# Two layers of a hybrid encoder on one core: the order in which four stages begin and end, bank pools of depth two, attention's tiles placed anew

## The chip, the cores and the metric

The kernel runs on one core of a Trainium2 chip. The time is that of one execution on the device in microseconds; a time is given as the median of several runs with the lowest and the highest. The engines are TensorE (PE, with PEld for its weight loads), VectorE (DVE), ScalarE (ACT), GpSimd (POOL) and SyncE (SP), whose queue issues the DMA transfers here. Each works through its own queue in order and waits on semaphores for the others.

## The reference, cut to what matters

1024 prompt rows and 128 sample rows of width 1024 pass one HGRN2 layer and one layer of differential attention, each followed by an MLP with squared ReLU; every part has a norm ahead of it and one behind.

```python
def _sqrelu_mlp(x, w_up, w_down):
    return jnp.square(jax.nn.relu(x @ w_up)) @ w_down
...
for l in range(DEPTH):
    a = _rmsnorm(h, norm_g[l, 0])
    if l < N_A_LAYERS:
        m, s_new = _hgrn2(a, hg_state0[l], w_hgrn_in[l], lb_all[l], hgrn_onorm_g[l], w_hgrn_out[l], is_prompt)
    else:
        kv = _rmsnorm(h, kv_norm_g) @ w_kv
        m = _diff_attn(a, k_new, v_new, past_k, past_v, w_q, lam_p, subln_g, w_o, l)
    h = h + _rmsnorm(m, norm_g[l, 1])
    f = _sqrelu_mlp(_rmsnorm(h, norm_g[l, 2]), w_up[l], w_down[l])
    h = h + _rmsnorm(f, norm_g[l, 3])
```

D_MODEL is 1024, the inner width of the MLP 4096, there are 8 heads of width 128 in either layer.

## The kernel before

The rows are cut into nine blocks of 128: 0 to 7 are the prompt (NBP is 8, NP is 4, half of it), 8 the sample. Every matrix product in full precision is made of three products of TensorE (`mm3`): each operand is split into a high part (a cast on ScalarE, `whi`, `aTh`, `s0h`, `wh`) and what is left (a subtraction on VectorE, `wlo`, `aTl`, `s0l`, `wl`).

The stages follow one another: the start (x is loaded, normalised, transposed), HGRN with its heads, its output projection (`out_proj`), the MLP of layer 0 (`mlp_up`, `mlp_down`), attention, its output projection, the MLP of layer 1. A scheduler sets the order of the instructions on every engine and interleaves the end of a stage with the start of the next, so a line that is moved in one place moves rows on all engines.

*Start.* The string `START` sets the order: x0 loads block 0 of x, n0 makes its root and scales it with `norm_x` (L311), W0 loads weight tile 0 and splits it (L189, L190), s36 makes one root for blocks 3 to 5. `rstd_of` makes a root: a step on VectorE (L203), a square root on ScalarE, then L205, L207 or L209 and L210, and L211 on VectorE. `pq`, `pf` and `pi` are the products of the first head; ScalarE makes the sigmoids `sg` of `pq` and `sf` of `pf`.

*Output projection and up stage.* In `out_proj` each block's product `pm` gets a norm, gain and residual (L654, L657), a norm and gain for the MLP (L275), and its transposes. `pair_sums` makes sums and differences of blocks j and j+4 (L675 to L678, four steps of 128x512), as the MLP's product is done by a Winograd scheme with seven products P1 to P7 for eight. In `mlp_up` the weights of a pair of column blocks get four sums (`sums`, L732 to L735, steps of 128x512) and splits (L718); the operands S1, S3 and S4 are halves of the blocks, transposed and split (`s_ops`), and only then the big tiles of the projection are given back (`keep.close()`). The pair i = 0 has an order of its own: `P1 P2 T ops P6 P5 P7 smp P3 P4`. P2 is added in the bank X of P1, so it waits until ScalarE has copied P1 out (L786).

*Down stage.* `mlp_down` runs seven passes over its products `D`; the last one, P4, has two parts: over the chunks c, then over the blocks j with 24 products each. A block that is done goes to `finish` (square sum `jk`, gain L977, root, residual L979) and in layer 0 through a second norm to `to_operand`, which transposes it on TensorE (`S<-ident,aO`). GpSimd makes the gains of the blocks in `POOL_MLP`, VectorE the others.

*Attention.* The weights of head pairs come through `load_w`, with a gain: a list of gains is applied per row group by ScalarE and VectorE, an array is multiplied in by GpSimd first (L188). `pj` is the product for K, V and Q; the tiles of the stage are placed by the string in `Area(as_, "at", ...)`, with two turns for those with a number.

Of the kernel before, what the change touches and what calls it, by code (L numbers as in the profile page):

```python
# [19 lines left out]
P = 128  # L20
# [24 lines left out]
START = 'x0 g x1 x2 n0 n1 n2 r W0 W1 x3 x4 x5 W2 W3 x6 x7 x8 s36 s69'  # L45
# [22 lines left out]
def tile_kernel(ctx, tc, x_prompt, x_sample, cache_k, cache_v, state_hgrn, norm_g, w_hgrn_in,  # L68
# [252 lines left out]
    for x in START.split():  # L321
# [4 lines left out]
        elif x[0] == "n":  # L326
            stats([int(x[1])])
            norm_x(int(x[1]))
# [277 lines left out]
    def out_proj(w, gains, gain, o_src, osc, g_post, h_old, h_new, g_pre, order, W=None, early={}):  # L606

        keep = ExitStack()
        ts, blk = Area(keep, "ts", "ss ss8 rs_v rs_y rs_t t:8"), {}
        with ExitStack() as os_:  # L610
# [4 lines left out]
            def block(b):  # L615
                blk[b] = (ts.tile([P, D], F32, name="t", bufs=NBP) if b < NBP
                          else pp.tile([P, D], F32, name="t8", bufs=1))
                return blk[b]
# [13 lines left out]
            for b in order:  # L632
# [30 lines left out]
                done.add(b)  # L663
                if b < NBP and b ^ NP in done:
                    pair_sums(blk, b % NP, nc.vector if len(done) == NBP else nc.gpsimd)
# [19 lines left out]
    def mlp_up(l, blk, keep):  # L685
        wu = w_up[l].rearrange("(k p) n -> p k n", p=P)
        with ExitStack() as ms, ExitStack() as ls:
            R = Area(ms, "ur", "wst s0h s0l s1h s1l a4h a1h a1l a3h a3l a4l p1 u2 u3 c0 hs", side="right")
            B = Area(ms, "ub", "X U Y:3 Z:3", space=PSUM)
# [4 lines left out]
            def bank(tag):  # L694
                return B.tile([P, 512], F32, name=tag, bufs=1 if tag in "XU" else 3)

# [6 lines left out]
            def s_ops(name, src):  # L703
# [4 lines left out]
                for j in range(NP):  # L708
                    c = slice(j * P, (j + 1) * P)
                    half_T(src(j), h[:, :, c], lo[:, :, c], transpose, lambda n: bank("YZ"[j % 2]))  # L710
# [18 lines left out]
            def sums(st):  # L729
                b11, b12, b21, b22 = [st[:, 4 * r:4 * r + 4, c * P:(c + 1) * P] for r in range(2) for c in range(2)]  # L730
                tt = nc.gpsimd.tensor_tensor
# [43 lines left out]
            sums(st)  # L775
            tset = pend = nx = None
            for i in range(NFP):
                sets = (raw, tset)
                C = {}
                seq = "P1 P2 T ops P6 P5 P7 smp P3 P4" if i == 0 else "P1 P6 P2 P5 P7 smp P3 P4"  # L780
                for op in seq.split():
# [7 lines left out]
                    elif op == "P2":  # L789
                        prod(X, op, sets, False)  # L790
                        c = C["c11"] = cell()
                        nc.scalar.activation(c, X, AF.Relu)
# [6 lines left out]
                    elif op == "ops":  # L799
                        s_ops("S1", lambda j: blk[j + NP][:, 512:D])  # L800
                        s_ops("S3", lambda j: blk[j + NP][:, 0:512])
                        s_ops("S4", lambda j: blk[j][:, 512:D])
# [12 lines left out]
                    elif op == "P7":  # L815
                        prod(Y, op, sets, False)
                        u3 = R.tile([P, HT], F32, name="u3", bufs=1)
                        add(out=u3, in0=Y, in1=p1, op=ALU.add)
                        c = C["c22"] = cell()
                        add(out=c, in0=Z, in1=u3, op=ALU.add)  # L820
                        relu2(c)
                        store(c, "A22", i)
                        if nx is not None:
                            raw = split(nx, 2 * i + 2, [(r0, ca), (r1, ca)])
                            sums(nx)
# [47 lines left out]
    def mlp_down(l, g_post, h_old, h_new, last):  # L873
        wd = w_down[l].rearrange("(i s p) n -> s p i n", s=2, p=P)
        NC = NFP // 2
        with ExitStack() as ms:
            L = Area(ms, "dl", "hst:3 aO")
            R = Area(rest, "dr", "wsta:3 aE gb wstb:2 sst:2 ysm jk wh:4 wl:4 hb:2 ss rs_v rs_y rs_t", side="right")
# [88 lines left out]
            def finish(b, y):  # L967
# [8 lines left out]
                ss = sumsq(y, jk, R)  # L976
                (nc.gpsimd if b in POOL_MLP else nc.vector).tensor_tensor(out=y, in0=y, in1=gain[0], op=ALU.mult)  # L977
# [12 lines left out]
                late.append((b, y, step[0]))  # L990

# [28 lines left out]
            for pi, (p, an, bn, sh) in enumerate(PASSES):  # L1020
# [7 lines left out]
                for c in range(NC // 2 if tail else NC):  # L1028
# [21 lines left out]
                    if late and late[0][2] < step[0] - 2:  # L1050
                        to_operand(*late.pop(0)[:2], s_bank)
                    if todo and c % 3 == 1:
# [7 lines left out]
                if tail:  # L1060
                    for j in range(NP):
# [6 lines left out]
                        while late and late[0][0] < NP + j - 1:  # L1068
# [10 lines left out]
    def next_stage(place):  # L1079

        for i, (b, hf, rs) in enumerate(left):
# [8 lines left out]
             norm_g[0:1, 2], "whix5 wlox5 whix6 wlox6 whix7 wlox7 gb:2 hb:2 t8")  # L1090
# [19 lines left out]
    with ExitStack() as as_:  # L1110
        ap = Area(as_, "at", "kt q2 k8 KS0 V0 pK KT_s qq pf px ws so Qx KS1")
        next_stage(ap.tile([P, 2, D], F32, name="KS1", bufs=1))
        ap.pool("V1")
# [42 lines left out]

        def loads(h):
# [358 lines left out]
```

## Time and profile before

| what | value |
|---|---|
| median of 3 runs | 2996.42 us (2992.04 to 2997.12) |
| profiled execution | 2992.95 us |
| its span | 2991.2 us |
| mean granted clock of TensorE | 0.986 |
| PE, DVE, ACT, POOL busy | 2869.2, 1855.1, 1198.1, 705.8 us |

The profile is of one execution. The span goes from the first to the last recorded instruction; the execution's own time is 1.75 us longer. Busy times add up an engine's instructions. A timeline row gives the start, the duration, engine, line, operation, the tile written and those read, and in brackets how long the engine had been idle and what ended that. A tile's number is left out.

### The profile page before, as it was taken

How to read it: one execution, taken by the hardware profiler on the slowest of the kernel's cores; microseconds unless marked ns; L12 is line 12 of the kernel's file. 1: busy time of each engine (PE TensorE's matmuls, PEld its weight loads, DVE VectorE, ACT ScalarE, POOL GpSimd, SP SyncE). 2: the span in 40 equal slices, each digit the busy share in tenths (PEclk: the TensorE clock that was granted, in tenths of full speed). 3: DMA queues.
4: the chain of work that ended last, by engine and by line, in shares of the span. 5: the costliest groups of instructions: out<-in, count | busy, mean ns of one | idle time of the engine just before them, and what ended most of it. 6: DMA issues, size and time to landing. Idle time of an engine off the chain costs nothing.

```text
span 2991.2 us, 45326 instructions
## 1 busy us (share of the span) xinstructions
PE 2869.2 (96%) x16897; PEld 2506.5 (84%) x16897; DVE 1855.1 (62%) x3480; ACT 1198.1 (40%) x2570; POOL 705.8 (24%) x578
## 2 busy tenths in 40 slices
PE   7999999989899999999989999998989999999997
PEld 7999999978788887887778999997868888878876
DVE  7777777767644445455856565656684444545566
ACT  5222222243433334343545454555543333444432
POOL 1111111102445440123021020110133454402130
PEclk9999999999999999999999999999999999999999
DMA  4111111142243348687732121212332443677776
GB/s 136 53 52 52 52 52 52 52 155 91 78 150 129 126 151 299 209 270 253 274 102 79 43 86 41 85 51 85 118 109 85 142 138 125 205 252 251 263 239 232
DMA packets 337120, 405.27 MB, mean 135 GB/s; under 512 B 21081, under 2 KB 210690, under 8 KB 336898
## 3 DMA queue, kind: packets, MB, share of 16 engines
q1 hardware_dynamic: 336898, 402.37, 40.9%
q8 instruction: 133, 2.18, 0.3%
q14 instruction: 89, 0.73, 0.1%
HBM read 280.12 MB, written 122.16 MB: 134 GB/s over the span
## 4 chain that ended last, share of the span: by engine, by line
PE 40%; DVE 6%; issue 2%; ACT 2%; DMA 2%; POOL 0%; SPq 0%; DVEq 0%; ACTq 0%; POOLq 0%
PE D L238 10%; PE pj L238 9%; PE Y L238 5%; PE Z L238 3%; PE X L238 3%; PE sc L238 2%; PE po L238 2%; PE S L238 1%; PE U L238 1%; PE pt L235 1%; DMA wsta<-in_w_down_dram 1%; DVE wl L891 1%; DVE rs_t L207 0%; DVE wlo L190 0%; PE pm L281 0%
## 5 line engine op out<-in xcount | busy, mean ns | idle before, releaser
L238 PE MATMUL D<-wh,aTh 128*128 128x512 f32 x896 | 357.2, 399 | 9.4 <-DVE aO L1007 6.3
L238 PE MATMUL D<-wl,aTh 128*128 128x512 f32 x896 | 355.7, 397 | 0.6 <-DVE wl L891 0.6
L238 PE MATMUL D<-wh,aTl 128*128 128x512 f32 x896 | 355.3, 397 | 0.0
L891 DVE TENSOR_TENSOR aTl<-hst,aTh 128x1024 fp32r<-128x1024 f32 x112 | 143.9, 1291 | 210.8 <-ACT aTh L890 210.7
L238 PE MATMUL pj<-whi,aTh 128*128 128x256 f32 x864 | 255.2, 295 | 13.5 <-DVE V L1190 13.0
L238 PE MATMUL pj<-wlo,aTh 128*128 128x256 f32 x864 | 244.5, 283 | 5.3 <-DVE wlo L190 5.3
L238 PE MATMUL pj<-whi,aTl 128*128 128x256 f32 x864 | 244.6, 283 | 0.0
L890 ACT CAST aTh<-hst 128x1024 fp32r<-128x1024 f32 x112 | 116.6, 1047 | 275.5 <-PE D L238 237.2
L238 PEld LDWEIGHTS D<-wh,aTh 128*128 128x128 f32 x896 | 170.3, 190 | 50.9 <-issue 6.7
L238 PEld LDWEIGHTS D<-wl,aTh 128*128 128x128 f32 x896 | 170.3, 190 | 40.1 <-DVE wl L891 1.1
L238 PEld LDWEIGHTS D<-wh,aTl 128*128 128x128 f32 x896 | 170.1, 190 | 39.6
L238 PEld LDWEIGHTS pj<-whi,aTh 128*128 128x128 f32 x864 | 164.1, 190 | 22.2 <-DVE V L1190 15.8
L238 PEld LDWEIGHTS pj<-wlo,aTh 128*128 128x128 f32 x864 | 164.1, 190 | 6.2 <-DVE wlo L190 5.5
L283 PE MATMUL pi<-whi,aTl 128*128 128x256 f32 x576 | 166.9, 290 | 0.0
L281 PE MATMUL pi<-whi,aTh 128*128 128x256 f32 x576 | 165.7, 288 | 0.6 <-ACT sf L423 0.6
L282 PE MATMUL pi<-wlo,aTh 128*128 128x256 f32 x576 | 165.9, 288 | 0.0
L238 PEld LDWEIGHTS pj<-whi,aTl 128*128 128x128 f32 x864 | 163.9, 190 | 0.0
L891 DVE TENSOR_TENSOR wl<-wsta,wh 128x1024 fp32r<-128x1024 f32 x112 | 148.7, 1330 | 22.4 <-ACT wh L890 19.3
L753 POOL TENSOR_TENSOR c<-c 128x512 f32<-128x512 f32 x96 | 115.0, 1198 | 163.9 <-ACT c L752 163.2
L752 ACT ACTIVATE c<-c 128x512 f32<-128x512 f32 x96 | 60.7, 632 | 231.5 <-DVE c L820 193.1
L890 ACT CAST wh<-wsta 128x1024 fp32r<-128x1024 f32 x112 | 117.2, 1048 | 64.5 <-PE D L238 23.5
L1271 POOL COPY qq<-q 128x256 f32<-128x256 f32 x64 | 29.4, 460 | 397.4 <-PE pqT L235 273.2
(475 smaller groups left out, 8048.3 us busy)
## 6 DMA issues: line engine op xcount, KB each, us to landing
u_dr<-c SPq DMA_DIRECT2D x224, 256.0 KB, 4.3
hst<-u_dr SPq DMA_DIRECT2D x112, 512.0 KB, 4.7
wsta<-in_w_down_dram SPq DMA_DIRECT2D x112, 512.0 KB, 5.4
wst<-in_w_up_dram SPq DMA_DIRECT2D x32, 1024.0 KB, 6.0
wstb<-in_w_down_dram SPq DMA_DIRECT2D x32, 512.0 KB, 5.1
t_dr<-wsta SPq DMA_DIRECT2D x32, 512.0 KB, 3.9
wstb<-t_dr SPq DMA_DIRECT2D x32, 512.0 KB, 5.8
h_dr<-hb SPq DMA_DIRECT2D x27, 512.0 KB, 2.6
```

The costliest lines, as they stand in the source:

```text
L235: pin(nc.tensor.transpose(out, in_, ident))
L238: pin(nc.tensor.matmul(*a, **k))
L281: matmul(out, lh, rh, start=first, stop=False)
L282: matmul(out, lh, rl, start=False, stop=False)
L283: matmul(out, ll, rh, start=False, stop=last)
L752: nc.scalar.activation(c, c, AF.Relu)
L753: nc.gpsimd.tensor_tensor(out=c, in0=c, in1=c, op=ALU.mult)
L890: nc.scalar.copy(h, st)
L891: vt(out=lo, in0=st, in1=h.bitcast(F32), op=ALU.subtract)
L1271: nc.gpsimd.tensor_copy(qq, view(Qb[h, i][:], (h % 2) * P, [(64, 2), (0, 2), (1, 64)]))
```

## The change

It has these parts.

- Start: blocks 1 and 2 of x share one root (`s13`), and are scaled one after the other behind it (`m1 m2`).
- Bank pools of the stages outside the MLP are written without the number of turns (pools with two buffers).
- `out_proj`: nine tiles `t` for nine blocks; the sample block's transposes leave the projection and come in `mlp_up` behind S4; the pair sums of the last three blocks run on VectorE, not only the last.
- `mlp_up`, first pair: P2 has a bank of its own and is added to P1's copy on VectorE; the operands come one by one between the products; the first weight sums run on VectorE; the operands' transposes get two banks of their own (T). In every pair the sum for c22 no longer has a tile u3.
- `mlp_down`, last pass: a block's second half gets its square sum and its gain ahead of the first; both `aO` blocks' transposes come behind the last block's products.
- Attention: weights of head 0 are scaled per row group; the tiles are placed anew.

```diff
-START = 'x0 g x1 x2 n0 n1 n2 r W0 W1 x3 x4 x5 W2 W3 x6 x7 x8 s36 s69'
+START = 'x0 g x1 x2 n0 s13 m1 m2 r W0 W1 x3 x4 x5 W2 W3 x6 x7 x8 s36 s69'
...
-        ps[0] = Area(banks[0], "ps", "mm:2 aux:2 wide:2", space=PSUM)
+        ps[0] = Area(banks[0], "ps", "mm aux wide", space=PSUM)
...
-                if b < NP or b == NBP:
+                done.add(b)
+                if b == NBP:
+                    continue
+                if b < NP:
                     half_T(t[:, 0:512], aTh[:, b, 0:4], aTl[:, b, 0:4])
...
-                    pair_sums(blk, b % NP, nc.vector if len(done) == NBP else nc.gpsimd)
+                    pair_sums(blk, b % NP, nc.vector if len(done) > NBP - 3 else nc.gpsimd)
...
-            B = Area(ms, "ub", "X U Y:3 Z:3", space=PSUM)
+            B = Area(ms, "ub", "X U Y:2 Z:2 T:2", space=PSUM)
...
-            sums(st)
+            sums(st, nc.vector)
...
-                seq = "P1 P2 T ops P6 P5 P7 smp P3 P4" if i == 0 else "P1 P6 P2 P5 P7 smp P3 P4"
+                seq = "P1 P2 T S1 P6 S3 P5 S4 P7 smp P3 P4" if i == 0 else "P1 P6 P2 P5 P7 smp P3 P4"
...
-                        prod(X, op, sets, False)
                         c = C["c11"] = cell()
-                        nc.scalar.activation(c, X, AF.Relu)
+                        if i == 0:
+                            V = bank("Z")
+                            prod(V, op, sets, True)
+                            add(out=c, in0=V, in1=p1, op=ALU.add)
+                            nc.scalar.activation(c, c, AF.Relu)
+                        else:
+                            prod(X, op, sets, False)
+                            nc.scalar.activation(c, X, AF.Relu)
...
+                if b in half:
+                    ss = sumsq(y[:, 0], jk[:, 0], R)
+                    nc.vector.tensor_tensor(out=y[:, 0], in0=y[:, 0], in1=gain[0][:, 0], op=ALU.mult)
+                    nc.vector.tensor_tensor(out=ss, in0=ss, in1=half[b], op=ALU.add)
...
+            def second_half(b, y):
+
+                jk = R.tile([P, 2, 512], BF16, name="jk", bufs=1)
+                half[b] = R.tile([P, 1], F32, name="sh", bufs=NP)
+                nc.scalar.activation(jk[:, 0], y[:, 1], AF.Square, accum_out=half[b])
+                nc.gpsimd.tensor_tensor(out=y[:, 1], in0=y[:, 1], in1=gain[0][:, 1], op=ALU.mult)
...
-                        while late and late[0][0] < NP + j - 1:
+                        while late and (late[0][0] < NP or j == NP - 1):
                             to_operand(*late.pop(0)[:2], s_bank)
...
-        ap = Area(as_, "at", "kt q2 k8 KS0 V0 pK KT_s qq pf px ws so Qx KS1")
+        ap = Area(as_, "at", "q2 kt so KS0 V1 pf px ws KT_s V0 k8 Qx KS1")
...
-                gs = view(gv[:], G_KV + 4 * kh, [(1, 4), (0, 2 * P)])
+                gs = per_row(G_KV + 4 * kh) if h == 0 else view(gv[:], G_KV + 4 * kh, [(1, 4), (0, 2 * P)])
```

How the rows stand on the engines now is shown at three places; a row has the line, the operation, the tile written and those read.

VectorE at the start, before (xb_233 is block 1 of x, `wlo` the first weight tile's low part):

```order
L207 SCALAR_TENSOR_TENSOR rs_t<-rs_y,rs_v 128x1
L211 SCALAR_TENSOR_TENSOR rs_y<-rs_t,rs_y 128x1
L311 SCALAR_TENSOR_TENSOR xb_233<-xb_233,rs_y,g_229 128x1024
L203 TENSOR_SCALAR rs_v<-ss 128x1
L372 COPY tv<-pv 128x41
L265 TENSOR_TENSOR aTl<-pt,aTh 128x512 x2
L373 COPY gv<-tv 128x24
L374 TENSOR_SCALAR gv<-tv 128x1
L376 TENSOR_TENSOR mx<-tv 128x8
L190 TENSOR_TENSOR wlo<-wst,whi 128x1024
```

The same stretch after (xb_224 and xb_226 are blocks 1 and 2):

```order
L205 RECIPROCAL rs_y<-rs_y 128x2
L381 TENSOR_TENSOR e_412<-tv,mx 128x8 x2
L190 TENSOR_TENSOR wlo<-wst,whi 128x1024
L209 TENSOR_TENSOR rs_t<-rs_y 128x2
L190 TENSOR_TENSOR wlo<-wst,whi 128x1024
L210 TENSOR_TENSOR rs_t<-rs_t,rs_v 128x2
L211 SCALAR_TENSOR_TENSOR rs_y<-rs_t,rs_y 128x2
L311 SCALAR_TENSOR_TENSOR xb_224<-xb_224,rs_y,g_220 128x1024
L311 SCALAR_TENSOR_TENSOR xb_226<-xb_226,rs_y,g_220 128x1024
L203 TENSOR_SCALAR rs_v<-ss 128x3
```

Block 1's scaling stood ahead of both `wlo` rows, and now stands behind them with block 2's.

TensorE at the end of the down stage of layer 0, before (the products D of the last two blocks, and `pj`, attention's first product):

```order
L238 MATMUL D<-wl,aTh 128x512
L238 MATMUL D<-wh,aTl 128x512
L235 MATMUL S<-ident,aO 128x128 x8
L238 MATMUL D<-wh,aTh 128x512
...
L238 MATMUL D<-wl,aTh 128x512
L238 MATMUL D<-wh,aTl 128x512
L235 MATMUL S<-ident,aO 128x128 x8
L238 MATMUL pj<-whi,aTh 128x256
```

After, from the last products D to the first `pj`:

```order
L238 MATMUL D<-wh,aTl 128x512
L238 MATMUL D<-wh,aTh 128x512
L238 MATMUL D<-wl,aTh 128x512
L238 MATMUL D<-wh,aTl 128x512
L235 MATMUL S<-ident,aO 128x128 x16
L238 MATMUL pj<-whi,aTh 128x256
L238 MATMUL pj<-wlo,aTh 128x256
L238 MATMUL pj<-whi,aTl 128x256
```

The first eight transposes stood 24 products ahead of the second eight, and now all sixteen stand behind the last product.

VectorE at the start of the up stage of layer 1, before (L718 are the splits of the weights, L654, L657 and L275 steps of the projection):

```order
L654 SCALAR_TENSOR_TENSOR t<-pm,rs_y,gb 128x1024
L657 TENSOR_TENSOR hb<-hb,t 128x1024
L718 TENSOR_TENSOR s0l<-wst,s0h 128x4x128 x4
L203 TENSOR_SCALAR rs_v<-ss 128x1
L247 TENSOR_TENSOR aTl<-pt,aTh 128x512 x2
L205 RECIPROCAL rs_y<-rs_y 128x1
L207 SCALAR_TENSOR_TENSOR rs_t<-rs_y,rs_v 128x1
L211 SCALAR_TENSOR_TENSOR rs_y<-rs_t,rs_y 128x1
L275 SCALAR_TENSOR_TENSOR t<-hb,rs_y,gb 128x1024
L718 TENSOR_TENSOR s1l<-wst,s1h 128x1024
```

After (L735 to L738 are the four weight sums, L721 the splits, L655 and L658 the projection's):

```order
L721 TENSOR_TENSOR s0l<-wst,s0h 128x4x128
L658 TENSOR_TENSOR hb<-hb,t 128x1024
L721 TENSOR_TENSOR s0l<-wst,s0h 128x4x128 x3
L735 TENSOR_TENSOR wst<-wst 128x4x128
L247 TENSOR_TENSOR aTl<-pt,aTh 128x512
L203 TENSOR_SCALAR rs_v<-ss 128x1
L247 TENSOR_TENSOR aTl<-pt,aTh 128x512
L736 TENSOR_TENSOR wst<-wst 128x4x128
L205 RECIPROCAL rs_y<-rs_y 128x1
L737 TENSOR_TENSOR wst<-wst 128x4x128
L207 SCALAR_TENSOR_TENSOR rs_t<-rs_y,rs_v 128x1
L738 TENSOR_TENSOR wst<-wst 128x4x128
```

The four weight sums were in GpSimd's queue, and now stand between VectorE's splits and evictions.

## Rows read from the trace of the kernel before

**Rows 1.** The page's section 1: busy time (share of span), instructions.

```profile
PE 2869.2 (96%) x16897; PEld 2506.5 (84%) x16897; DVE 1855.1 (62%) x3480; ACT 1198.1 (40%) x2570; POOL 705.8 (24%) x578
```

**Rows 2.** Waits of PE: tile, line, releaser: us, times, longest.

```profile
PE pt L235 <- ACT junk L1344: 6.4, 5, 1.7
```

**Rows 3.** Timeline, DVE, start: start, duration (us), instruction, [idle before, releaser].

```profile
15.59 1.23 DVE L190 TENSOR_TENSOR wlo<-wst,whi 128x1024 fp32r<-128x1024 f32 x1 [0.96 <-ACT whi L189]
...
18.43 1.29 DVE L311 SCALAR_TENSOR_TENSOR xb<-xb,rs_y,g 128x1024 f32<-128x1024 f32 x1
...
21.14 0.18 DVE L205 RECIPROCAL rs_y<-rs_y 128x3 f32<-128x3 f32 x1 [1.11 <-ACT rs_y L204]
...
21.82 0.68 DVE L265 TENSOR_TENSOR aTl<-pt,aTh 128x512 fp32r<-128x512 f32 x1
22.42 3.67 DVE L311 SCALAR_TENSOR_TENSOR xb<-xb,rs_y,g 128x1024 f32<-128x1024 f32 x3
```

**Rows 4.** Timeline, PE, start.

```profile
22.56 0.69 PE L282 MATMUL pq<-aTl,whi 128*128 128x384 f32 x1
...
33.46 0.39 PE L281 MATMUL pi<-whi,aTh 128*128 128x256 f32 x1 [0.64 <-ACT sf L423]
```

**Rows 5.** Timeline, ACT, start.

```profile
29.97 1.28 ACT L415 ACT_TABLE_LOAD   x1
...
32.93 0.48 ACT L423 ACTIVATE sf<-pf 128x384 f32<-128x384 f32 x1
35.64 1.05 ACT L189 CAST whi<-wst 128x1024 fp32r<-128x1024 f32 x1 [2.23 <-DMA wst<-in_w_hgrn_in_dram]
```

**Rows 6.** Timeline, PE, up stage of layer 0, its start.

```profile
763.25 0.79 PE L238 MATMUL X<-aTh,s0h 128*128 128x512 f32 x1 [5.01 <-ACT p L786]
...
773.13 1.94 PE L242 MATMUL pt<-ident,t 128*128 128x128 f32 x8 [4.25 <-DVE t L275]
```

**Rows 7.** Timeline, DVE, the same place.

```profile
760.51 1.67 DVE L675 TENSOR_TENSOR t<-t 128x512 f32<-128x512 f32 x1
...
764.68 0.69 DVE L677 TENSOR_TENSOR t<-t 128x512 f32<-128x512 f32 x1
```

**Rows 8.** Windows: stretch, busy us (instructions) by engine, PEclk, DMA share, GB/s.

```profile
757.00:763.00 6.00, 1.24 (x8) 0.76 (x6) 6.00 (x9) 2.96 (x5) 3.86 (x3) 0.85 0.00 0
763.00:768.00 5.00, 4.75 (x11) 3.79 (x12) 5.00 (x7) 0.19 (x1) 0.00 (x0) 0.50 0.51 153
```

**Rows 9.** Timeline, PE, up stage of layer 1, its start.

```profile
2243.53 1.94 PE L242 MATMUL pt<-ident,t 128*128 128x128 f32 x8 [6.61 <-DVE t L275]
...
2255.36 0.47 PE L238 MATMUL Y<-aTh,s1h 128*128 128x512 f32 x1 [2.27 <-DVE a3l L247]
```

**Rows 10.** Windows, the same place, columns as in rows 8.

```profile
2240.00:2249.00 9.00, 4.92 (x22) 4.55 (x23) 4.77 (x10) 3.66 (x8) 0.00 (x0) 0.50 0.14 58
```

**Rows 11.** Timeline, PE, end of the down stage of layer 0, start of attention.

```profile
1491.92 0.50 PE L238 MATMUL D<-wl,aTh 128*128 128x512 f32 x1 [0.63 <-DVE wl L891]
...
1510.66 1.97 PE L235 MATMUL S<-ident,aO 128*128 128x128 f32 x8 [5.25 <-ACT aO L989]
...
1520.48 1.10 PE L235 MATMUL S<-ident,aO 128*128 128x128 f32 x8 [0.90 <-ACT aO L989]
...
1531.30 0.58 PE L238 MATMUL pj<-wlo,aTh 128*128 128x256 f32 x1 [5.29 <-DVE wlo L190]
```

**Rows 12.** Timeline, DVE, the same place.

```profile
1524.98 2.01 DVE L211 SCALAR_TENSOR_TENSOR rs_y<-rs_t,rs_y 128x1 f32<-128x1 f32 x1
```

**Rows 13.** Timeline, POOL, the same place.

```profile
1524.61 2.37 POOL L977 TENSOR_TENSOR aO<-aO,gb 128x1024 f32<-128x1024 f32 x1
```

**Rows 14.** Timeline, PE, end of layer 1.

```profile
2933.90 0.77 PE L238 MATMUL D<-wh,aTh 128*128 128x512 f32 x1 [6.29 <-DVE aO L1007]
```

**Rows 15.** Timeline, DVE, end of layer 1.

```profile
2930.74 1.28 DVE L979 SCALAR_TENSOR_TENSOR hb<-aE,rs_y,hb 128x1024 f32<-128x1024 f32 x1
...
2983.88 1.77 DVE L207 SCALAR_TENSOR_TENSOR rs_t<-rs_y,rs_v 128x1 f32<-128x1 f32 x1
```

More of the change, by code (lines that the diff above doesn't have):

```diff
@@ L327, in tile_kernel @@
             stats([int(x[1])])
+            norm_x(int(x[1]))
+        elif x[0] == "m":
             norm_x(int(x[1]))
@@ L608, in out_proj @@
         keep = ExitStack()
-        ts, blk = Area(keep, "ts", "ss ss8 rs_v rs_y rs_t t:8"), {}
+        ts, blk = Area(keep, "ts", "ss ss8 rs_v rs_y rs_t t:9"), {}
         with ExitStack() as os_:
@@ L615, in block @@
             def block(b):
-                blk[b] = (ts.tile([P, D], F32, name="t", bufs=NBP) if b < NBP
-                          else pp.tile([P, D], F32, name="t8", bufs=1))
+                blk[b] = ts.tile([P, D], F32, name="t")
                 return blk[b]
@@ L694, in bank @@
             def bank(tag):
-                return B.tile([P, 512], F32, name=tag, bufs=1 if tag in "XU" else 3)
+                return B.tile([P, 512], F32, name=tag, bufs=1)
             def a_op(name, k):
@@ L709, in s_ops @@
                     c = slice(j * P, (j + 1) * P)
-                    half_T(src(j), h[:, :, c], lo[:, :, c], transpose, lambda n: bank("YZ"[j % 2]))
+                    half_T(src(j), h[:, :, c], lo[:, :, c], transpose, lambda n: bank("T"))
             def split(st, n, parts):
@@ L798, in mlp_up @@
                         nx = load(1)
[L799 to L802, printed above, removed]
+                    elif op == "S1":
+                        s_ops(op, lambda j: blk[j + NP][:, 512:D])
+                    elif op == "S3":
+                        s_ops(op, lambda j: blk[j + NP][:, 0:512])
+                    elif op == "S4":
+                        s_ops(op, lambda j: blk[j][:, 512:D])
+                        for z in range(2):
+                            half_T(blk[NBP][:, z * 512:(z + 1) * 512], aTh[:, NBP, 4 * z:4 * z + 4],
+                                   aTl[:, NBP, 4 * z:4 * z + 4], transpose, lambda n: bank("T"))
                         keep.close()
@@ L816, in mlp_up @@
                         prod(Y, op, sets, False)
-                        u3 = R.tile([P, HT], F32, name="u3", bufs=1)
-                        add(out=u3, in0=Y, in1=p1, op=ALU.add)
                         c = C["c22"] = cell()
-                        add(out=c, in0=Z, in1=u3, op=ALU.add)
+                        add(out=c, in0=Y, in1=p1, op=ALU.add)
+                        add(out=c, in0=c, in1=Z, op=ALU.add)
                         relu2(c)
@@ L824, in mlp_up @@
                             raw = split(nx, 2 * i + 2, [(r0, ca), (r1, ca)])
-                            sums(nx)
+                            sums(nx, nc.gpsimd)
                     elif op == "smp":
@@ L990, in finish @@
                 late.append((b, y, step[0]))
+            half = {}
+            def second_half(b, y):
[3 more added lines that the diff above has]
+                nc.gpsimd.tensor_tensor(out=y[:, 1], in0=y[:, 1], in1=gain[0][:, 1], op=ALU.mult)
             def evac(p, j, o):
@@ L1051, in mlp_down @@
                         to_operand(*late.pop(0)[:2], s_bank)
+                    if tail:
+                        second_half(NP + c, aO[:, :, c])
                     if todo and c % 3 == 1:
@@ L1155, in tile_kernel, with per_row @@
         WT, ready = {}, set()
+        def per_row(g):
+            return [gv[:, g + i:g + i + 1] for i in range(4)]
         def loads(h):
```

21 lines of the change are left out of this document (10 added, 11 removed).

## The prediction

> **What bounds the kernel now.** I read the busy shares first: TensorE works 96% of the span, VectorE 62%, ScalarE 40%, GpSimd 24% [rows 1]. So nothing that is only work on another engine matters; time can come from the few places where TensorE stands still, and from what its clock loses behind a standstill. The second view is therefore TensorE's waits, and the third the timeline around each of the longer ones. Four places concern this change. At the start VectorE normalises the rows of x one block after another [rows 3] before the products `pq` and `pi` can run through [rows 4]. At the start of each up stage TensorE waits 5.01 and 4.25 us in layer 0 [rows 6], 6.61 and 2.27 us in layer 1 [rows 9]. At the end of layer 0's down stage and the start of attention it waits four times, 0.63, 5.25, 0.90 and 5.29 us [rows 11]. At the end of layer 1 it waits 6.29 us for an add of VectorE [rows 14]. A standstill also costs clock: after the 5.01 us in layer 0 the granted clock was 0.50, the 1.2 GHz level, over the next 5 us [rows 8].
>
> The profiled execution took 2992.95 us, 1.75 us of it outside the span, and is 3.5 us under the median of the three runs. I work on the profiled one and put the sum on the median.
>
> **The change part by part.**
>
> *Start, a loss.* Blocks 1 and 2 of x now share one root. In VectorE's new order the roots and the scaling of block 1 stand behind the `wlo` splits of the first two weight tiles; the second of these ran at 15.59 for 1.23 us, to 16.82 [rows 3]. Block 2 was scaled at 18.43 already, so it moves little; block 1, which was scaled ahead of the splits, now is scaled beside it, and all four evictions of blocks 1 and 2 queue behind. Ahead of block 2's first one now stand the root of blocks 3 to 5, which cannot start before ScalarE's answer at 21.14, the three small steps behind it (to about 21.9), three scalings that took 3.67 together [rows 3], and block 1's second eviction, 0.6: 21.9 + 3.7 + 0.6 = 26.2 instead of 21.82. `pq` needs that eviction for its second kind of product, which ran at 22.56 [rows 4]; it now runs at about 26.3, +3.8. In ScalarE's queue the casts of the next head's weights now stand ahead of the table load and the two sigmoids `sg` and `sf`. The second cast waited for its weights until 35.64 and took 1.05 [rows 5], so they start at about 36.6; the load takes 1.28 and a sigmoid 0.48, to 38.9, and the first `pi`, which waits on `sf`, comes at about 39.3 instead of 33.46 [rows 4, 5]. That is +5.8, and TensorE is full from there through HGRN, so it isn't regained. I take **+6**, from +4 (only the first shift counts) to +9 (the second weight tile's split is later too).
>
> *Two-buffer bank pools outside the MLP, HGRN's end, the output projection.* The pools keep their depth of two; TensorE doesn't wait for a bank there in the rows of its waits. **0**, from −1.5 to +2.
>
> *Up stage of layer 0.* The second product P2 now has a bank of its own, so it no longer waits for ScalarE's copy `p` of P1 (5.01 us, [rows 6]). But the next thing in TensorE's order is the transposes of a half that the pair sums make on VectorE, and these, L677 among them, ran until 765.37 [rows 7]; from 757 to 763 VectorE was busy 6.00 of 6.00 us [rows 8]. The change adds to that queue: three of four pair sums (four steps each) and the first weight sums (four steps) leave GpSimd for VectorE. Against this, VectorE's own steps there get shorter without GpSimd beside them: L675 took 1.67 us, where its like, L677, took 0.69 [rows 7]. Counting VectorE's new queue with 0.60 for such a step, L677 ends at about 764.05, so that TensorE stands from 758.1 to 764.1, 6.0 instead of 5.01, P2 runs at half clock as now, and behind it come three waits of 1 to 3 us instead of the 4.25. P7, the product after the operands, then starts where it started, by that count 0.2 us later. **0**, −3 to +3.
>
> *Up stage of layer 1.* The same code, other neighbours: no step of GpSimd stretches VectorE's here, and the long waits are the later ones, 6.61 for `t` of the last block's scaling and 2.27 for `a3l` [rows 9], with the half clock after the first: 0.50 from 2240 to 2249, where TensorE was busy 4.92 us [rows 10], half of it, 2.4, lost. In the new order the sample block's transposes, for which the 6.61 was waited, come only behind the operands S1, S3 and S4, and these have banks of their own (T). By the same count as in layer 0, P2 waits for L677 some 4.6 us, and the small waits behind it come to 1.6 more than the small ones of now: 6.61 + 2.27 + 2.4 = 11.3 off, 4.6 + 1.6 on. **−5**, −8 to −1.
>
> *Down stage of layer 0 into attention.* Two edits meet. The transposes of two blocks of `aO` now both stand behind the last block's 24 products, instead of one ahead of them. And the weights of the first head are scaled row by row by ScalarE and VectorE, not by GpSimd ahead of them. The 0.63 us went with GpSimd's scaling. The 5.25 us wait goes, the products close up, and the last ends at about 1510.6. Then the second block's operand is late instead: it was there at 1520.48 [rows 11]. The second halves of the sums of squares and of the gains now go ahead, and VectorE's small steps are no longer held as the 128x1 one of 2.01 us beside GpSimd's gain of 2.37 [rows 12, 13]; I put the operand at about 1516.7, a new wait of some 4 to 6 us. The 5.29 us for `wlo` shrinks to about 1.3, if the `w_dq` weights land as they did. Sum: 0.63 + 5.25 + 0.90 + 5.29 = 12.1 off, 5 + 1.3 on. **−6**, −11 (no new wait for the operand) to −1 (operand and weights as late as now: 12.1 off, 1520.5 − 1512 = 8 to 9 and 2 to 3 on).
>
> That four half-gains of `aO` are now GpSimd's in each down stage is a cost the rows only hint at. They show the pattern: a 128x1 step of VectorE with two inputs in SBUF took 2.01 us while GpSimd multiplied for 2.37 [rows 12, 13]. The Trainium skill, "SBUF — State Buffer", section "Who interferes with whom", says that the pair of ports which VectorE shares with GpSimd is an exclusive lock: an instruction of VectorE with two SBUF inputs and a reading one of GpSimd block each other for the whole instruction. The trace agrees here. By that rule the four halves could hold VectorE 4 x 1.2 = 4.8 us in each down stage, an estimate from half of GpSimd's 2.37, and that is the second rival below.
>
> *Attention's tiles and the output projection of layer 1.* TensorE's transposes of `p` wait on `junk` of ScalarE five times, 6.4 us together [rows 2]. The tile of these transposes takes its two banks in the other turn now, so that three of these waits end with an earlier release; I take 0.45 off each, −1.3, and −0.7 at attention's end, where tiles are placed anew. **−2**, −5 to +2 (a placed-anew tile that waits for an older one's reader).
>
> *End of layer 1.* The add that TensorE waited 6.29 us for stood behind one scaling with residual of 1.28 us [rows 14, 15], which now comes after it: −1.2. The last block's root was held 1.77 us [rows 15] beside a gain of GpSimd, which the halves take away: −1.3. The extra gains of GpSimd in the stretch before cost 0 to 3; I take 1. **−1.5**, −3.5 to +2.
>
> Sum: 6 + 0 + 0 − 5 − 6 − 2 − 1.5 = −8.5. On the median: 2996.4 − 8.5 = **2988**.
>
> **The rivals.** *More gain (2982).* If VectorE's queue in layer 0 closes up more than I count (each step beside GpSimd stretched as L675 was, 1.67 for 0.69), L677 ends 2 to 3 us sooner, TensorE stands under 4 us, P2 runs at full clock (2.5 us), and the up stage of layer 0 gives what layer 1's does: −14. For it: VectorE had no idle time there [rows 8], so every stretched step was paid. Against: as many steps come on as are relieved.
>
> *The tail gives little (2993).* GpSimd's half-gains hold VectorE 4.8 us, the second `aO` operand comes as late as before, and only the closing-up is left: −6 becomes −1, total −3.5, which is no difference that can be measured. For it: the rows of a step held 2.01 us; against: there are fewer GpSimd steps in that stretch altogether, since the weights' gains left it.
>
> *Slower (3003).* The eight VectorE steps that move there per up stage, and the two more sets of four ahead of them, cost TensorE in full: VectorE is the engine that ends its waits in both up stages, and 757 to 763 had no gap [rows 8]. Sixteen steps of 0.60 are 9.6 us. If two thirds lie ahead of L677, layer 0 costs +6 and layer 1, with its −5 gone, +4: 6 + 6 + 4 − 6 − 2 − 1.5 = +6.5. It decides from the point at which the pair sums of blocks 1 and 2 no longer fit beside the projection's products. Against: those products left VectorE waits there, and the relief on L675 is in the rows.
>
> **How the numbers follow.** Forecast 0.52, more gain 0.20, tail 0.16, slower 0.12. About 0.2%, 6 us, is what a measurement of this kernel can tell from no change, so the border to "faster" is 2990.4 and to "slower" 3002.4. The forecast's own spread of some 6 us puts 0.38 of its 0.52 under the border, 0.13 between, 0.01 above. With the rivals: faster 0.38 + 0.20 + 0.02 = 0.60, same 0.13 + 0.14 + 0.01 = 0.28, slower 0.01 + 0.11 = 0.12. The range runs from 2976, six under the greater gain's 2982, to 3000, where only the slower rival lies outside.
>
> **What would show it.** Start: the first `pi` at about 39 instead of 33.5; at 35 or under, the loss isn't there. Layer 0's up stage: TensorE's first wait names a VectorE step of the pair sums, not `p`, and is about 6 us; P7 at the same distance from X's first product as now. Layer 1's: no wait over 5 us. Tail: no `aO` wait among the D products, one of 4 to 6 behind them, `wlo` under 2. End: the D wait about 5 us, no root over 0.3 us. What would make me wrong: next-head weights that land earlier at the start, `w_dq` weights that land later in the tail, or VectorE held by GpSimd's halves in the down stages, which would show as D products that wait for `wl`.

## The result, and the profile after

The changed kernel takes 2962.1 us (2961.3 to 2965.4), the kernel before 2996.8 over the runs beside it; the ratio is 0.9889, with a 95% interval of 0.9872 to 0.9906. That is 33 us less by the ratio and 35 by the medians, where the forecast was 8.5 less and the range ended 14 us above the result. Direction and most of the steps came as forecast; one step, put down at zero, was worth more than all the others together.

The head of the page after, and its busy times:

```profile
span 2959.5 us, 45358 instructions
...
PE 2862.0 (97%) x16897; PEld 2502.0 (85%) x16897; DVE 1848.0 (62%) x3523; ACT 1207.4 (41%) x2597; POOL 673.0 (23%) x558
```

TensorE is 7.2 us less busy than before [rows 1], on the same number of instructions, and its share of the span is 97%. The rest of the 31.7 us that the span lost is standstill. The largest waits of TensorE after (total, times, longest, in us):

```profile
PE pt L242 <- DVE t L680: 10.5, 2, 5.8
PE pt L255 <- DVE xb L311: 8.5, 1, 8.5
...
PE S L235 <- ACT aO L1007: 5.6, 1, 5.6
PE D L238 <- DVE aO L1034: 5.0, 2, 4.3
...
PE pt L235 <- ACT junk L1375: 3.1, 4, 1.1
```

Gone is the wait that stood at the head of the same view before:

```profile
PE pj L238 <- DVE V L1190: 13.0, 9, 1.8
```

To see where the time went I set the start of the same instruction of TensorE in both traces side by side. A row says how late the changed kernel (or an experiment) is against the kernel before at that instruction, in us; the difference of two rows is what the stage between them won or lost. In the text these rows go by the short names `pi`, `pm`, `U`, `pj` and `D`. Each kernel has one profile, and a single stage is good to some 3 us: e4, which leaves attention as it was, shows it 2.6 us shorter than before.

| TensorE's instruction | before, at | changed | e1, banks alone | e2, changed without banks |
|---|---|---|---|---|
| first `pi` (start) | 33.46 | +5.45 | +0.47 | +5.28 |
| last `pi<-whi` (HGRN) | 614.50 | +2.68 | −2.80 | +5.05 |
| 382nd `pm`, 12 us ahead of the last of layer 0 | 742.12 | +2.63 | −3.80 | +3.03 |
| first `U<-s0h,aTl` (up stage's first pair, layer 0) | 790.79 | +6.93 | −3.41 | +9.98 |
| first `S<-aE` (late in the down stage) | 1443.07 | +7.41 | −5.06 | +10.34 |
| 17th `pj<-wlo` (attention's start) | 1535.73 | +0.55 | −2.10 | +3.50 |
| last `pj<-whi` (attention) | 2061.07 | −18.92 | −21.67 | −0.20 |
| last `pm<-whi` of layer 1 | 2225.80 | −25.36 | −22.01 | −1.16 |
| first `U<-s0h,aTl` of layer 1 | 2265.49 | −29.61 | −21.96 | −3.54 |
| last `D<-wh,aTh` | 2980.29 | −30.78 | −22.34 | −3.49 |

Between attention's start and its last `pj` alone the changed kernel wins 19.5 us. There the same products read like this before (TensorE's timeline; its last row is the one that waited, and below it stands VectorE's copy of V):

```profile
1617.35 0.71 PE L235 MATMUL pt<-ident,p 128*128 128x128 f32 x5
1617.82 0.36 PE L238 MATMUL pj<-whi,aTh 128*128 128x256 f32 x1
...
1618.50 0.28 PE L238 MATMUL pj<-whi,aTl 128*128 128x256 f32 x1
1620.34 0.38 PE L238 MATMUL pj<-whi,aTh 128*128 128x256 f32 x1 [1.57 <-DVE V L1190]
...
1620.01 0.28 DVE L1190 COPY V<-pj 128x128 f32<-128x128 f32 x1
```

and after:

```profile
1615.39 0.72 PE L235 MATMUL pt<-ident,p 128*128 128x128 f32 x5
1615.87 0.37 PE L238 MATMUL pj<-whi,aTh 128*128 128x256 f32 x1
...
1616.55 0.28 PE L238 MATMUL pj<-whi,aTl 128*128 128x256 f32 x1
1616.66 0.28 PE L238 MATMUL pj<-whi,aTh 128*128 128x256 f32 x1
...
1618.04 0.28 DVE L1221 COPY V<-pj 128x128 f32<-128x128 f32 x1
```

The product at 1620.34 waited 1.57 us for VectorE's copy of V out of the product right ahead of it. After, its like at 1616.66 follows the row at 1616.55 with nothing between, 1.4 us ahead of that copy: it no longer writes the tile that the copy still has to read.

### The profile page after: what moved, and what is told of

It is laid out like the page before. It is cut to its first block, busy times and chain, and to the rows that moved or that the text cites. A ratio compares the mean times of both kernels' runs of the same rounds, so it can differ in the third digit from the quotient of the medians.

```text
span 2959.5 us, 45358 instructions
## 1 busy us (share of the span) xinstructions
PE 2862.0 (97%) x16897; PEld 2502.0 (85%) x16897; DVE 1848.0 (62%) x3523; ACT 1207.4 (41%) x2597; POOL 673.0 (23%) x558
## 4 chain that ended last, share of the span: by engine, by line
PE 39%; DVE 6%; DMA 3%; issue 2%; ACT 2%; POOL 0%; SPq 0%; DVEq 0%; ACTq 0%; POOLq 0%
PE pj L238 9%; PE D L238 8%; PE Y L238 4%; PE Z L238 3%; PE X L238 3%; PE sc L238 2%; PE po L238 2%; PE U L238 1%; PE S L238 1%; DMA wsta<-in_w_down_dram 1%; PE pt L235 1%; DVE wl L904 1%; PE pm L281 0%; DVE hb L997 0%; PE pm L282 0%
```

## The experiments

The theory that I formed from this: the bank pools did it (A). The rival: the new places of attention's tiles did it (B), since V1 is among the tiles that moved. Twelve kernels were run; the times are medians, the ratios are to the kernel before beside them.

### The bank pools

**e1**, the kernel before with the bank pools alone:

```diff
-        ps[0] = Area(banks[0], "ps", "mm:2 aux:2 wide:2", space=PSUM)
+        ps[0] = Area(banks[0], "ps", "mm aux wide", space=PSUM)
```

> The kernel before with one edit: the bank pools outside the MLP as two-buffer pools (mm, aux, wide) instead of two turns each. Theory A (a two-buffer pool hands out the bank that was given back first, strict turns hand out the older one): TensorE's nine waits of pj for the copy of V, 13.0 us, go, the waits on junk shrink by about 3 us, HGRN and the second output projection gain some 2 to 6 us more: 2996 falls by 18 to 24 us. Theory B (the placing of attention's tiles did that, the banks nothing): within 2 us of before, the nine waits still there.

Measured: 2973.8 us, ratio 0.9926 (0.9914 to 0.9939), 21 us less. The nine waits are gone, and of the waits on `junk` half is left:

```profile
PE pt L235 <- ACT junk L1344: 3.2, 4, 1.1
```

**e2**, the changed kernel with that line as before:

> The changed kernel with the turns of before put back for mm, aux and wide. Theory A: it loses what the banks gave, 18 to 24 us of the changed kernel's gain of 34, and the waits of pj for V are back with about 13 us; the start's loss no longer shrinks from 5.4 to 2.7 us through HGRN. Theory B: within 3 us of the changed kernel.

Measured: 2987.7 us, ratio 0.9973 (0.9961 to 0.9985). The waits are back, at nearly their old size:

```profile
PE pj L238 <- DVE V L1221: 12.7, 9, 1.8
...
PE pt L235 <- ACT junk L1375: 6.4, 5, 1.7
```

Theory B has fallen: without the pools the rest of the change, tiles included, is 7 to 8 us. That is close to the 8.5 that the prediction gave for all of it.

**e3**, the kernel before with the pool for `mm` alone, `"mm aux:2 wide:2"`:

> The kernel before with the two-buffer pool for mm alone, aux and wide in turns. Theory A with the price at pj: 12 to 14 us less than before, the waits on junk (6.4 us) stay. If the gain is that of all three pools (18 to 24), the junk waits were the projections' doing; if it is under 5, the banks of aux or wide carry it.

Measured: 2981.5 us, ratio 0.9953 (0.9940 to 0.9967). No wait of `pj` for V is listed, and the one on `junk` stands:

```profile
PE pt L235 <- ACT junk L1344: 6.0, 4, 1.7
```

**e9**, the kernel before with the pool for `aux` alone, `"mm:2 aux wide:2"`:

> The kernel before with the two-buffer pool for aux alone. The three pools together gave 21 us, mm alone 13. Theory A (the transposes pt and the small tiles of attention get the bank that was given back first): the waits on junk, 6.4 us, fall by some 3, and the 3.3 us by which HGRN was shorter with all three pools are aux's too: 5 to 8 us less than before. Rival: these belong to wide or only come together with mm: within 3 us of before.

Measured: 2989.7 us, ratio 0.9983 (0.9974 to 0.9992). Here it is the other way round:

```profile
PE pj L238 <- DVE V L1190: 12.9, 9, 1.8
...
PE pt L235 <- ACT junk L1344: 3.4, 5, 1.1
```

So 13 to 14 us are the bank of `pj`, 5 to 7 the banks of the small tiles, and they add up to e1's 21. On top of the other edits the same line gives more, 25 us (the changed kernel against e2): 15.8 in attention, 5.5 in the second output projection, 2.7 in the up stage of layer 0 and 2.5 in HGRN. Of e9's gain 2.9 us arise in HGRN, like e1's 2.8 (the last `pi` comes at 611.57 and 611.70 instead of 614.50), while with `mm` alone it comes at 614.72. So HGRN's part belongs to `aux`. Which instructions of HGRN got shorter I can't say: TensorE's list of waits names none there over 0.6 us in either trace.

What the pools change is which bank the next tile gets. With two turns, `pj`, `kps` (the four transposes of `stack`, which fall into the middle of a projection) and the next `pj` get first, second, first: the product must wait until VectorE has copied V out of the product right ahead of it. In eight of the nine places TensorE's timeline has the four `kps` inside the product right ahead of the one that waits. With the pool that one starts ahead of the copy, as the rows above show, so it has another bank. That a two-buffer pool gives out the bank that was given back first is my reading of this; e3 shows that the line does it, and at which wait.

### Where attention's tiles lie

**e8**, the changed kernel with the string of places as before:

```diff
-        ap = Area(as_, "at", "q2 kt so KS0 V1 pf px ws KT_s V0 k8 Qx KS1")
+        ap = Area(as_, "at", "kt q2 k8 KS0 V0 pK KT_s qq pf px ws so Qx KS1")
...
+        ap.pool("V1")
```

> The changed kernel with attention's tiles placed as before. Theory A: no wait of pj for V comes back, within 2 us of the changed kernel between attention's start and its end; what the placing gave is at attention's end and in the output projection, at most 4 us. Theory B (tiles carry it): 10 us or more lost.

Measured: 2969.3 us, ratio 0.9909 (0.9893 to 0.9926), 5 to 7 us more than the changed kernel. At the last `pj` it is 2.6 us ahead of the changed kernel, so inside attention the places cost nothing; at the last `pm` of layer 1 it is 5.6 behind. The second output projection thus gives 8.2 us, twice what I had allowed at most. The queue of SyncE shows what happens there. Its issues of the last weights of the projection and of the first of the up stage, in e8:

```profile
2119.27 0.38 SPq L174 DMA_DIRECT2D wst<-in_w_do_dram  x1
...
2128.50 0.38 SPq L729 DMA_DIRECT2D wst<-in_w_up_dram  x1
```

and in the changed kernel:

```profile
2103.75 0.38 SPq L174 DMA_DIRECT2D wst<-in_w_do_dram  x1
...
2119.53 0.43 SPq L729 DMA_DIRECT2D wst<-in_w_up_dram  x1
```

The first is issued 15.5 us earlier, the second 9. As I read it, both go to tiles that lie where attention's tiles lay, and wait for the last reader of what was there. The kernel before issued them at 2134.35 and 2144.20, 73 and 83 us behind its last `pj`; the changed one does so 62 and 77 behind, e8 80 and 89. What these loads give isn't separated. Of the 8.2 us, 1.8 come within 20 us of the last `pj`, ahead of these loads, where the mean granted clock over 25 us was 0.80 in e8 and 0.93 in the changed kernel. The other 6.4 come among the projection's own products, where TensorE waits 5.5 us in all for steps of VectorE in e8, and 1.0 in the changed kernel; that VectorE is earlier there because the weights come earlier is not shown. And the places give this only together with the pools: in e2, which has the new places and the old turns, the second projection is just 1.0 us shorter than before.

### The start

**e5**, the changed kernel with the start of before (`n0 n1 n2` instead of `n0 s13 m1 m2`):

> The changed kernel with the start of before (blocks 1 and 2 of x with a root each). Theory A (the start's shift of 5.4 us lasts, and the shrinking to 2.7 through HGRN is the bank pools' gain): 5 us less than the changed kernel, 2957. Rival (HGRN takes the shift up, TensorE waits there less when it is late): 2 to 3 us less, or nothing.

Measured: 2955.9 us, ratio 0.9861 (0.9846 to 0.9876). The first `pi` comes 4.8 us earlier than in the changed kernel, the last one 5.4, the last `D` 5.9. The rival, that HGRN takes the shift up, has fallen; e2 says the same, whose shift was 5.28 at the first `pi` and 5.05 at the last.

### The up stage of layer 0

**e4**, the kernel before with only the edits of the up stage and of the projection's end:

> The kernel before with only the edits of the up stage and of the output projection's end (own bank for P2, T banks, operands between the products, nine tiles t, pair sums and first weight sums on VectorE). By the changed kernel's trace: +4 us in the up stage of layer 0, -4 in layer 1's, sum within 2 us of before. If the prediction's count were right: 0 and -5. Rival: the second output projection's gain (about -4 between attention's end and the up stage) is from the nine tiles t, then -4 to -6 in all.

Measured: 2996.8 us, ratio 1.0008 (0.9999 to 1.0017): nothing. By the landmarks it is 7.2 us later in the up stage of layer 0 (−0.25 at the 382nd `pm`, +6.96 at the first `U`) and 3.1 earlier in layer 1's (+10.51 to +7.38). Its profile is of an execution 5 us above its median. But e2, whose profile is near its median, loses 7.0 in the same stage, and the kernels with the pools (e5, e8, e10, e11) 3.8 to 4.4 like the changed one: without the pools the up stage of layer 0 costs 7 us, with them 4.

**e6**, the changed kernel, layer 0's up stage as before, layer 1's as changed (each edited place asks for the layer; two of them):

```diff
-            sums(st, nc.vector)
+            sums(st, nc.vector if l else nc.gpsimd)
...
-                        if i == 0:
+                        if i == 0 and l:
                             V = bank("Z")
```

> The changed kernel with the up stage of layer 0 as before (order of the first pair, P2 in P1's bank, no T banks, sums and pair sums on GpSimd, sample block's transposes in the projection), layer 1 as changed. Theory A (the edits lose 4 to 7 us in layer 0 by the pair sums and by the half clock behind three waits, and win 4 in layer 1): 4 to 7 us less than the changed kernel, 2956. By the prediction's count, 0 within 3 us.

Measured: 2957.8 us, ratio 0.9870 (0.9855 to 0.9885), 4 us less than the changed kernel; the gain stands between the 382nd `pm` (−0.5) and the first `U` (−4.8). The nine tiles `t` and the sum without u3 stay in both layers.

**e7**, both of them, the old start and the old up stage of layer 0:

> The two of them together. If the two losses add: 9 to 12 us less than the changed kernel, 2951. If the time gained is given back at the down stage's weights or at attention's start, 5 or less.

Measured: 2951.6 us, ratio 0.9851 (0.9836 to 0.9866), the lowest of all the medians (e5's interval overlaps with it): 10 us less than the changed kernel. At the first `U` the two add up in full, 10.5 us; at attention's start 8.4 are left and at the last `D` 6.9. The profiled runs' spans differ by 7.2 (2952.3 against 2959.5).

**e12**, the changed kernel with the old start, and in layer 0 only the first weight sums back on GpSimd (`sums(st, nc.vector if l else nc.gpsimd)`):

> The changed kernel with the start of before, and in layer 0 only the first weight sums back on GpSimd (four steps of 128x512; VectorE runs them in 0.68 each). Theory A (VectorE's queue ahead of the pair sums sets the wait there): the wait for L680's like falls from 5.8 by 2 to 3 us, and the up stage of layer 0 ends 2 to 4 us earlier than with old start alone (2956). Rival (GpSimd beside VectorE stretches the steps by as much): within 1.5 us, steps of VectorE over 1 us where 0.68 was.

Measured: 2957.3 us, ratio 0.9872 (0.9854 to 0.9889); e5 has 2955.9. The rival holds. TensorE's wait for the pair sum is 5.98 us, with another of 1.43 ahead of it, not 3 (5.79 in e5). VectorE's timeline says why:

```profile
751.83 2.41 DVE L275 SCALAR_TENSOR_TENSOR t<-hb,rs_y,gb 128x1024 f32<-128x1024 f32 x1
...
754.22 2.23 DVE L719 TENSOR_TENSOR s1l<-wst,s1h 128x1024 fp32r<-128x1024 f32 x1
...
757.76 1.21 DVE L719 TENSOR_TENSOR s1l<-wst,s1h 128x1024 fp32r<-128x1024 f32 x1
```

The step L275 took 2.41 us and the first split L719 2.23, the second 1.21. GpSimd in the same stretch:

```profile
751.87 1.28 POOL L735 TENSOR_TENSOR wst<-wst 128x512 f32<-128x512 f32 x1 [0.69 <-DVE rs_y L211]
753.23 2.13 POOL L736 TENSOR_TENSOR wst<-wst 128x512 f32<-128x512 f32 x1
```

Each long step of VectorE lies beside a sum of GpSimd, as L675 did before [rows 7, 8]. What VectorE loses by taking the sums, four steps of 0.68, it loses about as much of beside GpSimd when it doesn't: 2.1 us in these two steps alone. This is the exclusive port pair that the Trainium skill states ("SBUF — State Buffer", section "Who interferes with whom"), and the trace agrees: 2.23 against 1.21 for two halves of the same split.

### The end of the down stage

**e10**, the changed kernel with the last pass of the down stage as before:

```diff
-                    if tail:
-                        second_half(NP + c, aO[:, :, c])
...
-                        while late and (late[0][0] < NP or j == NP - 1):
+                        while late and late[0][0] < NP + j - 1:
```

> The changed kernel with the down stage's last pass as before (no halves ahead, one block's transposes among the products). The prediction put the last pass and the weights' scaling at -6 together and layer 1's end at -1.5. If the order of the transposes and the halves carry it: 4 to 6 us more than the changed kernel, with aO waits of 5 and 1 us among the products. If the weights' scaling carries it: within 2 us.

Measured: 2968.0 us, ratio 0.9912 (0.9896 to 0.9928), 6 us more than the changed kernel. The place of the old transposes is back, with 4.27 us of waiting for `aO` among the products, and the wait for `wlo` is 4.52 us instead of 2.26. By attention's start 3.7 us are lost (from −0.88 at the 225th `D` to +2.86 at the 17th `pj<-wlo`, against the changed kernel), 2.6 of them behind the first `S<-aE`. Another 2.6 are lost in the up stage of layer 1, which this edit doesn't touch: TensorE waits 9.1 us there and 9.4 in the changed kernel, but the mean granted clock of the stage is 0.86 instead of 0.95. Behind the last `D` 1.4 us are lost (3.8 there, 5.2 in the span), where the last block's square sum and gain are whole again.

**e11**, the changed kernel with the first head's weights scaled by GpSimd, as before:

> The changed kernel with the first head's weights scaled by GpSimd as before. If this edit shortened the wait of pj for wlo (5.3 to 2.3 us): 2 to 4 us more than the changed kernel, all of it at attention's start. Rival: the weights' landing sets that wait, then within 1 us.

Measured: 2963.9 us, ratio 0.9895 (0.9880 to 0.9911): no difference that can be measured. The wait for `wlo` grows from 2.26 to 4.35 us, but the one for the second block of `aO` falls from 5.62 to 3.90, and after attention's start 1 us is left. The waits of the place, with the 0.71 for `wl` that the changed kernel has and e11 hasn't, come to 8.6 us there and 8.3 here. As I read it, they feed on the same queue of VectorE, and who is served first only decides which of them TensorE sees.

## Why the prediction was wrong

| step | forecast | measured, from the landmarks |
|---|---|---|
| start | +6 | +5.5 |
| bank pools up to layer 0's projection | 0 (−1.5 to +2) | −2.8 |
| up stage of layer 0 | 0 (−3 to +3) | +4.3 |
| down stage into attention | −6 | −6.9, with +0.5 ahead of it |
| attention, second projection | −2 (−5 to +2) | −25.9 |
| up stage of layer 1 | −5 | −4.3 |
| end of layer 1 | −1.5 | −2.1 |
| sum | −8.5 | −31.7 |

**Bank pools: the step that failed.** "The pools keep their depth of two; TensorE doesn't wait for a bank there in the rows of its waits. 0." The rows say otherwise. The first row of TensorE's waits was the 13.0 us of `pj` for the copy of V. V isn't read by `pj`: the copy reads `pj`. A product that waits for the instruction that empties a tile of its own name is a product that waits for a bank. The prediction doesn't name this row at all; it judges the edit by the depth of the pools, not by the order in which banks are given out. e1, e2, e3 and e9 put 21 to 26 us on that line: about 14 on `mm`, 5 to 7 on `aux`, of which HGRN's 2.8, and up to 5 more together with the other edits. The junk waits fell too, by 3 us and not by the 1.3 that I had: from 6.4 [rows 2] to 3.4 with the pool for `aux` alone.

**Attention's tiles: a gain, far too small.** I took 0.7 for the places and named only a tile that waits as the risk. With the new places the weights of the next stages are issued 15.5 and 9 us earlier; together with the pools the places were worth 8.2 us in the second projection, 5 to 7 us of the time (e8). By what path isn't shown.

**Start: right.** VectorE's timeline follows the working row by row:

```profile
15.71 1.23 DVE L190 TENSOR_TENSOR wlo<-wst,whi 128x1024 fp32r<-128x1024 f32 x1 [1.19 <-ACT whi L189]
...
17.24 2.48 DVE L311 SCALAR_TENSOR_TENSOR xb<-xb,rs_y,g 128x1024 f32<-128x1024 f32 x2
...
22.07 1.28 DVE L311 SCALAR_TENSOR_TENSOR xb<-xb,rs_y,g 128x1024 f32<-128x1024 f32 x1
23.27 0.68 DVE L265 TENSOR_TENSOR aTl<-pt,aTh 128x512 fp32r<-128x512 f32 x1
23.87 2.47 DVE L311 SCALAR_TENSOR_TENSOR xb<-xb,rs_y,g 128x1024 f32<-128x1024 f32 x2
26.26 0.69 DVE L265 TENSOR_TENSOR aTl<-pt,aTh 128x512 fp32r<-128x512 f32 x1
```

Block 1's and 2's scaling runs at 17.24 behind the second split, and the eviction that I put at 26.2 came at 26.26. ScalarE's second cast, table load and sigmoids came at 35.41 to 38.64, close to the working. The first `pi` came at 38.91, forecast 39.3, instead of 33.46 [rows 4]; it waited 0.45 us. And it isn't regained: the 2.8 us by which the shift shrinks through HGRN are the bank pools' (e1, e2, e5).

**Up stage of layer 0: the wait right, its price too low.** TensorE's rows there:

```profile
766.69 1.09 PE L242 MATMUL pt<-ident,t 128*128 128x128 f32 x4 [5.79 <-DVE t L680]
767.43 0.78 PE L238 MATMUL Z<-aTh,s0h 128*128 128x512 f32 x1
...
791.34 1.94 PE L235 MATMUL T<-ident,t 128*128 128x128 f32 x8 [3.20 <-DVE a4l L247]
792.93 0.78 PE L238 MATMUL Y<-a3h,s1h 128*128 128x512 f32 x1
```

The first wait is 5.79 us for the pair sum L680 (forecast 6.0, L677 by the old numbers), and the last of the operand waits 3.20 (forecast 1 to 3). The windows (busy us by PE, PEld, DVE, ACT, POOL, then the clock) show what I left out:

```profile
767.00:772.00 5.00, 5.00 (x15) 4.04 (x14) 3.95 (x9) 1.94 (x4) 0.00 (x0) 0.50 0.94 313
772.00:788.00 16.00, 12.71 (x75) 9.90 (x73) 9.03 (x13) 7.49 (x13) 1.04 (x1) 0.98 0.05 18
788.00:797.00 9.00, 5.80 (x20) 4.84 (x19) 4.94 (x6) 2.63 (x5) 6.23 (x5) 0.62 0.00 0
```

After either wait the granted clock was lower: 0.50, the 1.2 GHz level, from 767 to 772, and 0.50 again from the end of the second wait at 791.34 to 796.5 (the 0.62 of the last row also holds the standstill's start and P7's end). I had counted the first, under P2, and not the second, which falls on the last eight transposes of `T` (1.94 us; eight of them took 1.03 at 784.89) and the product P7: P7's first steps are 0.43 apart, and at full clock 0.23. P7 starts 35.9 us behind X's first product, 33.1 before, where I had 0.2 later, and takes 4.6 us instead of 2.7. So the stage is 4.3 us longer, above the +3 that I allowed. The wait of 3.20 stands behind VectorE too: two splits of weights, 2.36 us from 788.24, run ahead of the eviction at 790.51 that frees the bank.

The count of what moved was wrong as well. Not three of the four pair sums left GpSimd: VectorE ran one before and three after in layer 0, two after in layer 1. With the weight sums that is twelve steps and eight, not the sixteen of the "slower" rival. This rival had the mechanism, VectorE's queue ahead of the pair sums, and +6 for it; e4 alone has +7.2, the changed kernel +4.3. It didn't decide the sum. The rival of the greater gain counted on full clock behind a standstill of under 4 us; behind the 3.20 here the clock was at its lower level for 5 us.

**Up stage of layer 1: right.** The 6.61 and 2.27 us [rows 9] are gone; what is there:

```profile
2209.63 1.03 PE L242 MATMUL pt<-ident,t 128*128 128x128 f32 x4 [4.66 <-DVE t L680]
...
2229.72 1.25 PE L235 MATMUL T<-ident,t 128*128 128x128 f32 x8 [0.81 <-DVE a4l L247]
```

4.66 for the pair sum (forecast 4.6), and T waits of 0.5 to 1.5 behind it. The stage is 4.3 us shorter, forecast 5. The nine other profiles with these edits in layer 1 show 1.6 to 4.8, with 7.9 to 9.3 us of waits in each; the mean granted clock of the stage was 0.86 where it gained least and 0.95 where it gained most, so the 4.3 has some luck in it.

**Down stage into attention: the path right, the size half by luck.** One wait for `aO` stands behind the products, and a short one for `wlo`:

```profile
1523.03 1.97 PE L235 MATMUL S<-ident,aO 128*128 128x128 f32 x8 [5.62 <-ACT aO L1007]
...
1532.61 0.38 PE L238 MATMUL pj<-wlo,aTh 128*128 128x256 f32 x1 [2.26 <-DVE wlo L182]
```

5.62 us (forecast 4 to 6) and 2.26 (forecast 1.3), where four waits of 12.1 us were [rows 11]. The 0.63 for `wl`, which I took for gone with GpSimd's scaling, is still there as 0.71 at 1497.49. So the waits came to 8.6 us and not 6.3, and give 3.5 of the 6.9. The rest goes with the clock, which I left out here: from the first `S<-aE` to the 17th `pj<-wlo` its mean was 0.91 before and 0.95 after, and some 2 us of that stand right behind that `S<-aE`, at 0.50 and 0.81 in two stretches of 3 us before and at 1.00 after. The order of the transposes and the halves carry it (e10); the scaling of the weights, which I credited with the shorter `wlo` wait, gives 1 us at most (e11). The second rival, GpSimd's half-gains that hold VectorE 4.8 us, came in small: the four halves ran from 1468.76 to 1471.85 and from 1488.03 to 1491.69, beside them two 128x1 steps of VectorE (L211) took 0.97 and 1.25 us where others took 0.16, and the products waited only the 0.71. Between 1505 and 1524 us GpSimd has only two gains of weights, and beside the second of them a 128x1 step of VectorE (L207) took 1.79 us at 1521.93.

**End of layer 1: right.** The wait for the add fell from 6.29 [rows 14] to

```profile
2901.69 0.47 PE L238 MATMUL D<-wh,aTh 128*128 128x512 f32 x1 [4.33 <-DVE aO L1034]
```

4.33 us, 2.0 less instead of the 1.2 forecast.

So the sum of what was worked out came to 7 to 8 us in e2, close to the forecast, but by errors that cancel: +7.0 in layer 0's up stage where 0 was forecast, and against it −2.3 from the first `pi` to that stage (0 forecast) and −4.7 in attention and the second projection (−2 forecast). The 8.5 is wrong by a factor of four because one edit was set at nothing on a general ground, that the depth stayed the same, while the row that would have priced it stood at the head of the view.

## What to carry to other kernels

When a wait of an engine ends with the instruction that empties the very tile it is about to write, it is a wait for a buffer, and every edit on how buffers are given out must be priced at that row, even where their number stays. With strict turns of two, a tile that slips in between two others gives the second of them the buffer of the first, which may still be read; a pool of the same size, which as I read it gives out what was given back first, was worth 0.7% here. And a stage that pays in one layer may cost in another: the same edits were worth −4.3 us in layer 1 (−1.6 to −4.8 over the profiles) and +4.3 in layer 0, so that the version with the lowest median, 2951.6 us, keeps the old start and the old order in layer 0 and takes the rest.

## What the runs showed of the hardware

Moving the weight sums from VectorE back to GpSimd changed nothing that could be measured, in a stretch where both read SBUF: with the weight sums on GpSimd, VectorE's steps of 1.2 us took 2.2 to 2.4 beside them (e12), and the wait of TensorE was 7.4 us in all instead of 5.8 (e5). A standstill of TensorE of 3.20 us was followed by a granted clock of 0.50 for 5.2 us, as one of 5.79 was by 0.50 from 767 to 772; I had not expected it of the shorter one.
